# Stacked halves for decay and rate, and two reordered hand-ons, in an RWKV-7 / differential-attention trunk

## The chip, the cores and the metric

The kernel runs on one core of a Trainium2 chip. The metric is the device time of one launch in microseconds (us). Three runs of the kernel before gave 2142.01, 2142.14 and 2135.95 us, so their median is 2142.01. The profile is of one more execution, which took 2144.47 us; the trace of it spans 2142.8 us, with 1.67 us of the launch lying outside.

## The reference, cut to what matters

The program is a trunk of two layers on 512 tokens of 1024 channels in float32. Layer 0 is a feed-forward block, an RWKV-7 time mixing and another feed-forward block; layer 1 is the same with a differential attention in the middle. The change touches only the time mixing:

```python
r, k, v = jnp.einsum('sbtc,scd->sbtd', h[None] + dx[None] * mu[:3, None, None, :], w_rkv)
xw = h + dx * mu[3]; xa = h + dx * mu[4]; xg = h + dx * mu[5]
w_log = -jax.nn.softplus(-(w0 + jnp.tanh(xw @ w1) @ w2)) - 0.5
decay = jnp.exp(-jnp.exp(w_log))
a = jax.nn.sigmoid(a0 + (xa @ a1) @ a2)          # the "rate"
g = jax.nn.sigmoid(xg @ g1) @ g2                 # the gate, 160 inner channels
kk = (k * k_k).reshape(B, T, H, N)
kk = kk * lax.rsqrt(jnp.maximum(jnp.sum(kk * kk, axis=-1, keepdims=True), 1e-24))
k = k * (1 + (a - 1) * k_a)
y = wkv7_scan(heads(r), heads(decay), heads(k), heads(v), -kk, kk * a_h)   # heads of 64
```

w1, a1, w2 and a2 have an inner size of 64. Decay and rate are thus products over 64 channels, with 1024 outputs for each of 512 tokens.

## The kernel before, in words

Activations lie transposed: a tile has 128 channels on the partitions and the 512 tokens along the free axis, so 1024 channels are eight tiles, named 0 to 7. Every large product is computed in a split form. Each operand is cut into a high half (a cast to the 32-bit matmul format, by ScalarE) and a low half (the rest, a subtraction by VectorE), and `mm3` (lines 198 to 202) issues three matmuls of 512 columns for one product: high weights by high data (L200), high by low (L201), low by high (L202). Weights are cast at L146 and subtracted at L147 (`halves`), at L181/L182 (`wrows`, for the values) or at L194/L195 (`wflat`, for the small factors); activations at L207/L208 (`split`).

The program is traced with a tile scheduler. Within each engine it puts the instructions of independent pieces of the code into one fixed order before the launch, and each engine then runs its list strictly in that order; buffers come from pools with a fixed number of slots (`bufs`). `tc.issue_after(i)` tells this scheduler that what follows may not stand ahead of instruction `i`. The order on the chip is therefore a matter of the program alone, and an instruction that waits holds everything behind it in its list.

The time mixing runs in these steps, with their place in the trace of before:

- The low-rank inputs. `z` holds tanh(xw w1) on rows 0 to 63 and xa a1 on rows 64 to 127. Its halves are `zh`, `zl` (L603, L604). The gate's inner 160 channels are cut into 128 (`gh`, `gl`) and 32; the 32 go into a stacked tile `z3` of 96 rows.
- Decay, rate and gate, 400.75 to 417.66 us (loop from L674). For each of eight output tiles p and for each row half `hh` one `mm3` with 64 rows on both operands: rows 0 to 63 give decay, whose sigmoid goes to `A` (L681), rows 64 to 127 give rate, whose sigmoid goes to `BK` (L683). Three rounds later the gate's tile: one `mm3` of 128 rows and one 96-row matmul with `z3` (L689); VectorE copies the tile out of PSUM (L691).
- The mixing of v, k and r (`mixed`): for each of eight tiles a scaling of h (on VectorE at L654 for v, on ScalarE at L656 for k and r), a multiply-add on VectorE (L657), and a split (L207, L208).
- The values, 417.66 to 461 us, and beside them `rec(p)`, which turns decay into the factors of the recurrence: a scan on VectorE (L704) and more work on ScalarE and VectorE (L707 to L715).
- The key projection, from 461.3 us. `proj` (L209 to L251) computes two output tiles at a time from a block of 256 columns of the weights. When a tile is done it is put on the list `last`, and `hand_on` passes the tile that has waited there to the callback `done`. With `by_rows=b` the block at column b runs its products row by row, alternating between its two tiles. With `flush=False` the tile that is still on the list at the end is returned.
- The callback of the key projection is `key_done`: `key_cb` squares the tile on ScalarE (L755, into the tile `nacc`), a matmul with a block-diagonal matrix sums each head (L759), and a chain on ScalarE and VectorE normalises the key (L762 to L773, the last into `sA`). `scores(p - 2)` then moves a tile's rows into place by DMA (L786, `x<-sA`) and multiplies them (L794, L796). Last come steps of a triangular inversion on VectorE (`run(inv0, ...)`, L830 and L831).
- The receptance's projection R: its first block runs by rows with `feed(k)` between the products, which hands on key tile 7 and the scores of tiles 6 and 7. After it comes the recurrence proper (`wkv`).

## Time and profile before

| what | us |
|---|---|
| timed runs | 2142.01, 2142.14, 2135.95 |
| the profiled execution, and its span | 2144.47, 2142.8 |
| TensorE busy in the span | 2109.4 (98%) |
| VectorE, ScalarE busy | 1199.8 (56%), 816.7 (38%) |
| decay, rate and gate: TensorE from first to last start | 16.91 |
| gap between starts ahead of the first key tile's sum (L759) | 3.02 |
| gap between starts ahead of the last tile's scores (L794) | 1.75 |

How to read it: TensorE works nearly the whole span, so the time is the number of matmuls by their spacing, plus the places where TensorE stands. Matmuls are pipelined; the spacing of starts is what one costs, and the duration in a row is longer than that. The averages of the page hide the few places that the change touches, which the stretches and timelines show.

### The profile page before, as it was taken

What the parts mean: (1) busy time and instruction counts of PE and PEld (TensorE: products, weight loads), DVE (VectorE), ACT (ScalarE), POOL (GpSimd) and SP (SyncE); (2) the same over time, 40 slices, a digit from 0 to 9 for tenths busy, and PEclk for the clock granted to TensorE, in tenths of its full rate; (3) what the DMA queues carried; (4) which work ended last, traced back from release to release, by engine and by line L of the source; (5) the groups of instructions that cost most, each with busy time, mean ns of one, the idle gap of its engine ahead of it and who ended that gap; (6) DMA issues with size and microseconds to landing.
All of it is one profiled execution on the core that took longest, in us unless ns stands there. A gap on an engine that the chain in (4) does not pass through costs nothing.

```text
span 2142.8 us, 26517 instructions
## 1 busy us (share of the span) xinstructions
PE 2109.4 (98%) x10479; PEld 1771.9 (83%) x10479; DVE 1199.8 (56%) x1854; ACT 816.7 (38%) x1389; POOL 210.6 (10%) x250
## 2 busy tenths in 40 slices
PE   9999999999989999999999999999999999999999
PEld 7888888778789978888888988888889778888887
DVE  6644445797877764535446545445356855444443
ACT  5322223587235443323224342223235854222222
POOL 1100000000222201101000001001010210100000
PEclk9999999999989999999999999999999999999999
DMA  4333323346655542233223232333322113222222
GB/s 159 118 98 99 99 94 101 112 137 163 151 135 123 119 134 85 97 98 99 98 88 109 79 99 98 98 98 99 98 79 85 35 60 99 95 93 91 95 98 79
DMA packets 272920, 219.39 MB, mean 102 GB/s; under 512 B 85658, under 2 KB 257852, under 8 KB 272796
## 3 DMA queue, kind: packets, MB, share of 16 engines
q1 hardware_dynamic: 272796, 217.70, 33.5%
q8 instruction: 82, 1.34, 0.3%
q14 instruction: 42, 0.34, 0.0%
HBM read 193.02 MB, written 16.25 MB: 98 GB/s over the span
## 4 chain that ended last, share of the span: by engine, by line
PE 88%; DVE 6%; ACT 3%; DMA 1%; issue 1%; SPq 1%; POOL 0%; ACTq 0%; DVEq 0%
PE ps L200 27%; PE ps L202 27%; PE ps L201 27%; ACT s L1200 1%; PE ps L978 1%; PE ps L960 1%; PE ps L1004 1%; PE ps L966 1%; PE ps L993 1%; PE ps L988 0%; PE ps L972 0%; PE ps L995 0%; DVE wlo L147 0%; DVE s L1210 0%; DVE xmt L657 0%
## 5 line engine op out<-in xcount | busy, mean ns | idle before, releaser
L200 PE MATMUL ps<-xgh,whi 128*128 128x512 f32 x1688 | 658.4, 393 | 1.6 <-ACT whi L146 0.9
L201 PE MATMUL ps<-xgl,whi 128*128 128x512 f32 x1688 | 655.8, 390 | 0.0
L202 PE MATMUL ps<-xgh,wlo 128*128 128x512 f32 x1688 | 648.2, 390 | 0.1
L146 ACT CAST whi<-wraw 128x1024 fp32r<-128x1024 f32 (+2 forms) x296 | 303.5, 1030 | 880.3 <-PE ps L201 594.5
L147 DVE TENSOR_TENSOR wlo<-wraw,whi 128x1024 fp32r<-128x1024 f32 (+2 forms) x296 | 429.0, 1453 | 91.4 <-ACT whi L146 80.7
L200 PEld LDWEIGHTS ps<-xgh,whi 128*128 128x128 f32 x1688 | 316.4, 188 | 74.2 <-ACT whi L146 3.1
L201 PEld LDWEIGHTS ps<-xgl,whi 128*128 128x128 f32 x1688 | 316.9, 188 | 66.8 <-issue 1.7
L202 PEld LDWEIGHTS ps<-xgh,wlo 128*128 128x128 f32 x1688 | 316.6, 188 | 66.2 <-DVE wlo L147 0.6
L399 POOL TENSOR_TENSOR u<-u,g 128x512 f32<-128x512 f32 x88 | 124.7, 1418 | 1401.4 <-ACT whi L146 1114.4
L201 PE MATMUL ps<-actl,whi 128*128 128x512 f32 x656 | 255.2, 389 | 0.0
L200 PE MATMUL ps<-acth,whi 128*128 128x512 f32 x656 | 254.7, 389 | 0.0
L202 PE MATMUL ps<-acth,wlo 128*128 128x512 f32 x656 | 254.7, 389 | 0.0
L398 DVE TENSOR_TENSOR u<-ps,R 128x512 f32<-128x512 f32 x88 | 60.8, 691 | 286.6 <-PE ps L202 286.5
L441 DVE SCALAR_TENSOR_TENSOR x<-ps,x 128x512 f32<-128x512 f32 x88 | 60.5, 691 | 222.8 <-PE ps L202 222.8
L201 PEld LDWEIGHTS ps<-actl,whi 128*128 128x128 f32 x656 | 123.1, 188 | 25.6
L202 PEld LDWEIGHTS ps<-acth,wlo 128*128 128x128 f32 x656 | 123.1, 188 | 25.5
L200 PEld LDWEIGHTS ps<-acth,whi 128*128 128x128 f32 x656 | 123.1, 188 | 25.5
L200 PE MATMUL ps<-whi,xgh 128*128 128x256 f32 (+1 forms) x384 | 122.8, 323 | 0.2 <-DVE mx L1195 0.2
L201 PE MATMUL ps<-wlo,xgh 128*128 128x256 f32 (+1 forms) x384 | 122.5, 319 | 0.0
L202 PE MATMUL ps<-whi,xgl 128*128 128x256 f32 (+1 forms) x384 | 122.2, 318 | 0.0
L395 DVE TENSOR_TENSOR g<-ps,R 128x512 f32<-128x512 f32 x88 | 60.8, 691 | 108.2 <-PE ps L202 108.1
L207 ACT CAST acth<-u 128x512 fp32r<-128x512 f32 x88 | 54.8, 623 | 118.9 <-POOL u L399 118.8
(330 smaller groups left out, 2201.9 us busy)
## 6 DMA issues: line engine op xcount, KB each, us to landing
wraw<-in_ffn_w_in_dram SPq DMA_DIRECT2D x87, 1024.0 KB, 5.1
wraw<-in_ffn_w_out_dram SPq DMA_DIRECT2D x34, 1024.0 KB, 5.2
wraw<-in_rwkv_w_rkv_dram SPq DMA_DIRECT2D x12, 1024.0 KB, 5.7
wraw<-in_ffn_w_out_dram SPq DMA_DIRECT2D x12, 768.0 KB, 4.5
wraw<-in_w_kv_dram SPq DMA_DIRECT2D x8, 1024.0 KB, 5.0
am_d<-nsq SPq DMA_DIRECT2D x16, 256.0 KB, 2.9
AM<-am_d SPq DMA_DIRECT2D x16, 256.0 KB, 3.0
wraw<-in_diff_w_q_dram SPq DMA_DIRECT2D x4, 1024.0 KB, 5.4
```

The costliest lines, as they stand in the source:

```text
L146: self.nc.scalar.copy(hi[:, ks], raw[:, :, c : c + P])
L147: (eng or self.nc.vector).tensor_sub(lo[:, ks], raw[:, :, c : c + P], hi[:, ks].bitcast(F32))
L200: mm(ps, wh, xh, start=start, stop=False)
L201: mm(ps, wh, xl, start=False, stop=False)
L202: mm(ps, wl, xh, start=False, stop=stop)
L207: self.nc.scalar.copy(hi, src)
L395: nc.vector.tensor_mul(g, pg, self.R)
L398: nc.vector.tensor_mul(u, pu, self.R)
L399: nc.gpsimd.tensor_mul(u, u, g)
L441: nc.vector.scalar_tensor_tensor(x, ps, 0.5, x, ALU.mult, ALU.add)
L960: mm(pw[:, p, 0:L], Mo[:, p, :], DT[:, p, :].rearrange("p (h t) -> p h t", h=2)[:, :, 32:], start=True, stop=True)
L966: mm(p1[:, p, :], bbd[:, p, :], mv[:, p, :], start=True, stop=True)
```

## The change

There are three edits, in `proj`, in the decay and rate products, and in the mixing of the receptance.

The first: where the by-rows block is the last one and the list isn't flushed (the key projection), the two `hand_on` calls behind its products are left out, so two tiles, 6 and 7, stay on the list; `proj` returns the list, and `feed` hands on tile 6 at k = 0 and tile 7 at k = 1. (The call at k == 1 inside the by-rows loop, which hands on tile 5, stays.)

The second: the data tile for decay, `zw`, holds the high half of rows 0 to 63 of `z` on rows 0 to 63, and its low half on rows 64 to 127; `za` is the same for rate, the other way round. The weights `ww` hold the high half of w2 twice, one under the other, and `wa` that of a2. One matmul of 128 rows then gives high by high plus high by low, and one of 64 rows adds low by high. Three matmuls per product become two, 48 become 32. The weights of both are loaded twice, by two more DMAs, and there is one more cast of 128x1024 and one subtraction more of the weights; the split of `z` is two half-height copies and two half-height subtractions where there was one of each.

The third: ScalarE's scalings for the receptance may not stand ahead of the first key tile's square.

```diff
@@ proj
-                if not first or b:
+                if rows and not flush:
+                    pass
+                elif not first or b:
                     hand_on()
                 elif j == 0:
                     first()
                 last.append((b // P + j, pss[j]))
         if flush:
             hand_on()
-        return last[0] if last else None
+        return last
...
-            zh, zl = halves(z)
+            zw, za = (self.tl(self.gp, n, dt=F32R, bufs=XB) for n in ("xgh", "xgl"))
+            nc.scalar.copy(zw[half[0]], z[half[0]])
+            nc.vector.tensor_sub(zw[half[1]], z[half[0]], zw[half[0]].bitcast(F32))
+            nc.scalar.copy(za[half[1]], z[half[1]])
+            nc.vector.tensor_sub(za[half[0]], z[half[1]], za[half[1]].bitcast(F32))
...
-            def mixed(s, eng=None):
+            def mixed(s, eng=None, after=None):
...
-                        nc.scalar.activation(t, h[k][:, 1:], AF.Copy, scale=self.omu[:, i : i + 1])
+                        with tc.issue_after(after) if after else nullcontext():
+                            nc.scalar.activation(t, h[k][:, 1:], AF.Copy, scale=self.omu[:, i : i + 1])
...
-            wh, wl = self.wflat([(prm["w2"], 0), (prm["a2"], 64)], P)
+            ww, wa = (self.tl(self.wp, n, (P, 8, P), F32R, bufs=3).rearrange("p k f -> p (k f)") for n in ("whi", "wlo"))
+            wl = self.tl(self.wp, "wlo", (P, 8, P), F32R, bufs=3).rearrange("p k f -> p (k f)")
+            raw = self.tl(self.wp, "wraw", (P, 2, C), bufs=2)
+            for i, (w, n) in enumerate(((ww, "w2"), (wa, "a2"))):
+                for hh in half:
+                    nc.sync.dma_start(raw[hh, i], prm[n])
+                nc.scalar.copy(w, raw[:, i])
+                nc.vector.tensor_sub(wl[half[i]], raw[half[i], i], w[half[i]].bitcast(F32))
...
-            self.tl(self.wp, "wlo", (P, 8, P), F32R, bufs=3)
...
-                        self.mm3(ps, wh[hh, c], wl[hh, c], zh[hh], zl[hh], True, True)
+                        mm(ps, (ww, wa)[i][:, c], (zw, za)[i], start=True, stop=False)
+                        mm(ps, wl[hh, c], (zw, za)[i][hh], start=False, stop=True)
...
+            squares = []
+
             def key_cb(p, ps):
                 bb, kb = BK[:, p, :, 0:L], BK[:, p, :, L:]
                 sq = self.tl(self.gp, "nacc")
-                nc.scalar.activation(sq, ps, AF.Square, scale=self.v("k_k", p))
+                squares.append(nc.scalar.activation(sq, ps, AF.Square, scale=self.v("k_k", p)).ins)
...
-            xr = mixed(0)
+            xr = mixed(0, after=squares[0])

             def feed(k):
-                if k == 0:
-                    key_done(*last)
+                if k < 2:
+                    key_done(*last[k])
```

The lines below the edits move in the new file: L681, L683, L689 and L691 of before become L698, L700, L706 and L708; L755 and L759 become L774 and L778; L794 and L796 become L813 and L815; L656 and L657 become L665 and L666. The new products of decay and rate are L695 (128 rows) and L696 (64 rows).

TensorE's order within the decay, rate and gate stretch, before: rounds of three 64-row matmuls (data `xgh_2765`, `xgl_2766`), three 128-row matmuls of the gate (data `xgh_2800`), and the first two 96-row matmuls that finish a gate tile.

```order
L200 MATMUL ps_2920<-xgh_2800,whi_2850 128x512
L201 MATMUL ps_2920<-xgl_2801,whi_2850 128x512
L202 MATMUL ps_2920<-xgh_2800,wlo_2851 128x512
L200 MATMUL ps_2928<-xgh_2765,whi_2844 128x512
L201 MATMUL ps_2928<-xgl_2766,whi_2844 128x512
L202 MATMUL ps_2928<-xgh_2765,wlo_2845 128x512
L689 MATMUL ps_2902<-xgh_2834,whi_2854 128x512
L689 MATMUL ps_2920<-xgh_2834,whi_2854 128x512
L200 MATMUL ps_2933<-xgh_2765,whi_2844 128x512
```

The same place after, with the ninth decay and rate pairs; `wlo_2845` are the low weights, used with 64 rows.

```order
L695 MATMUL ps_2940<-xgh_2765,whi_2843 128x512
L696 MATMUL ps_2940<-xgh_2765,wlo_2845 128x512
L695 MATMUL ps_2944<-xgl_2766,wlo_2844 128x512
L696 MATMUL ps_2944<-xgl_2766,wlo_2845 128x512
L200 MATMUL ps_2948<-xgh_2802,whi_2857 128x512
L201 MATMUL ps_2948<-xgl_2803,whi_2857 128x512
L202 MATMUL ps_2948<-xgh_2802,wlo_2858 128x512
L706 MATMUL ps_2900<-xgh_2836,whi_2861 128x512
L706 MATMUL ps_2916<-xgh_2836,whi_2861 128x512
L706 MATMUL ps_2932<-xgh_2836,whi_2861 128x512
L706 MATMUL ps_2948<-xgh_2836,whi_2861 128x512
L695 MATMUL ps_2956<-xgh_2765,whi_2843 128x512
```

Each 64-row matmul (L696) now stands alone between matmuls of 128 rows, and the gate's first finishing matmul (L706 into `ps_2900`) has moved behind the decay and rate products of seven of the eight output tiles and behind four gate tiles' first three matmuls; before, its counterpart (L689 into `ps_2902`) stood behind those of five and a half output tiles and two gate tiles.

VectorE's order at the first copy of a gate tile, before: `xmt` are the mixing's intermediate tiles of v, `t_468` takes the gate's first tile.

```order
L644 TENSOR_TENSOR xgh_2834<-t_444_2828,xgh_2834 32x512
L208 TENSOR_TENSOR xgl_3010<-xmt_3006,xgh_3009 128x512
L208 TENSOR_TENSOR xgl_3017<-xmt_3013,xgh_3016 128x512
L654 TENSOR_SCALAR xmt_3020<-h_395_2578,omu 128x512
L654 TENSOR_SCALAR xmt_3027<-h_396_2579,omu 128x512
L691 COPY t_468_2907<-ps_2902 128x512
L657 SCALAR_TENSOR_TENSOR xmt_3020<-h_395_2578,vec_530,xmt_3020 128x512
L691 COPY t_472_2925<-ps_2920 128x512
```

And after:

```order
L652 TENSOR_TENSOR xgh_2836<-t_444_2830,xgh_2836 32x512
L208 TENSOR_TENSOR xgl_3000<-xmt_2996,xgh_2999 128x512
L708 COPY t_468_2905<-ps_2900 128x512
L708 COPY t_472_2921<-ps_2916 128x512
L208 TENSOR_TENSOR xgl_3007<-xmt_3003,xgh_3006 128x512
L662 TENSOR_SCALAR xmt_3010<-h_395_2578,omu 128x512
L662 TENSOR_SCALAR xmt_3017<-h_396_2579,omu 128x512
L666 SCALAR_TENSOR_TENSOR xmt_3010<-h_395_2578,vec_530,xmt_3010 128x512
```

The first copy of a gate tile stands three instructions earlier in the list of the mixing's work: ahead of one low half (`xgl_3007`) and of the two next scalings.

ScalarE's order around the first key tile's square, before: L656 are the receptance's scalings (`xmt_4048` and on), L146 a cast of weights, L755 the square into `nacc_3520`.

```order
L207 CAST xgh_3449<-xmt_3446 128x512
L207 CAST xgh_3456<-xmt_3453 128x512
L656 ACTIVATE xmt_4048<-h_393_2576,omu 128x512
L656 ACTIVATE xmt_4055<-h_394_2577,omu 128x512
L207 CAST xgh_4051<-xmt_4048 128x512
L207 CAST xgh_4058<-xmt_4055 128x512
L656 ACTIVATE xmt_4062<-h_395_2578,omu 128x512
L146 CAST whi_3547<-wraw_3541 128x1024
L755 ACTIVATE nacc_3520<-ps_3470,vec_530 128x512
L656 ACTIVATE xmt_4069<-h_396_2579,omu 128x512
```

And after, where the square is L774 into `nacc_3510` and the receptance's scalings are L665 into `xmt_3964` and on:

```order
L207 CAST xgh_3439<-xmt_3436 128x512
L207 CAST xgh_3446<-xmt_3443 128x512
L146 CAST whi_3537<-wraw_3531 128x1024
L774 ACTIVATE nacc_3510<-ps_3460,vec_530 128x512
L665 ACTIVATE xmt_3964<-h_393_2576,omu 128x512
L665 ACTIVATE xmt_3971<-h_394_2577,omu 128x512
L146 CAST whi_3668<-wraw_3666 128x1024
```

Between the key's last casts and the square there stands one cast of weights now, and no longer three scalings and two casts of the receptance beside it.

TensorE's order where the last key tile is handed on, before: L759 sums tile 7's heads, and the scores (L794, L796) and R's first products follow.

```order
L794 MATMUL ps_4010<-BK_2840,x_517_3065 128x128 x4
L796 MATMUL ps_4011<-ident,x_517_3065 128x128 x4
L759 MATMUL ps_4120<-nacc_4116,bd 128x512
L794 MATMUL ps_4136<-BK_2840,x_518_3066 128x128 x4
L796 MATMUL ps_4137<-ident,x_518_3066 128x128 x4
L794 MATMUL ps_4152<-BK_2840,x_518_3066 128x128 x4
L796 MATMUL ps_4153<-ident,x_518_3066 128x128 x4
L200 MATMUL ps_4114<-xgh_4051,whi_4106 128x512
```

And after, where that sum is L778 into `ps_4116`:

```order
L202 MATMUL ps_4031<-xgh_3981,wlo_4027 128x512
L200 MATMUL ps_4030<-xgh_3988,whi_4022 128x512
L201 MATMUL ps_4030<-xgl_3989,whi_4022 128x512
L778 MATMUL ps_4116<-nacc_4112,bd 128x512
L813 MATMUL ps_4132<-BK_2842,x_518_3056 128x128 x4
L815 MATMUL ps_4133<-ident,x_518_3056 128x128 x4
L813 MATMUL ps_4148<-BK_2842,x_518_3056 128x128 x4
```

The sum of tile 7 stands 20 of R's matmuls later than before; between tile 6's sum and it there now stand the scores of tile 4 and those 20.

## Rows read from the trace of the kernel before

**Rows 1.** The page: the span, and the chain that ended last by engine.

```profile
span 2142.8 us, 26517 instructions
...
PE 88%; DVE 6%; ACT 3%; DMA 1%; issue 1%; SPq 1%; POOL 0%; ACTq 0%; DVEq 0%
```

**Rows 2.** Stretches (us): length, each engine's busy time, TensorE's granted clock, DMA share, GB/s.

```profile
400.75:417.66 16.91, 16.27 (x82) 10.60 (x82) 12.88 (x22) 14.92 (x27) 0.00 (x0) 1.00 0.16 62
417.66:469.50 51.84, 51.84 (x229) 42.54 (x227) 51.73 (x71) 41.81 (x78) 1.92 (x2) 1.00 0.47 151
472.40:475.43 3.03, 0.40 (x3) 0.01 (x1) 2.72 (x4) 2.92 (x5) 0.48 (x2) 1.00 0.00 0
475.43:478.94 3.51, 3.51 (x7) 2.15 (x7) 3.12 (x5) 2.88 (x5) 0.00 (x0) 0.51 0.45 140
483.48:485.27 1.79, 1.79 (x7) 1.13 (x6) 1.55 (x3) 1.69 (x3) 0.00 (x0) 1.00 0.00 0
546.39:548.14 1.75, 0.39 (x3) 0.03 (x1) 1.69 (x5) 1.54 (x5) 0.00 (x0) 1.00 0.85 163
588.07:598.31 10.24, 9.41 (x44) 9.04 (x44) 8.22 (x23) 0.37 (x1) 0.00 (x0) 0.50 0.27 54
```

**Rows 3.** Timeline of TensorE, decay and gate: start, duration, line, tiles, shape, idle before.

```profile
400.75 1.19 PE L200 MATMUL ps<-xgh,whi 64*128 64x512 f32 x7
...
403.69 0.50 PE L200 MATMUL ps<-xgh,whi 128*128 128x512 f32 x1
404.03 0.40 PE L201 MATMUL ps<-xgl,whi 128*128 128x512 f32 x1
404.26 0.40 PE L202 MATMUL ps<-xgh,wlo 128*128 128x512 f32 x1
404.59 0.75 PE L200 MATMUL ps<-xgh,whi 64*128 64x512 f32 x2
...
406.63 0.50 PE L200 MATMUL ps<-xgh,whi 64*128 64x512 f32 x1
...
407.52 0.73 PE L689 MATMUL ps<-xgh,whi 96*128 96x512 f32 x2
408.89 0.50 PE L200 MATMUL ps<-xgh,whi 64*128 64x512 f32 x1 [0.64 <-ACT BK L683]
```

**Rows 4.** Timeline of VectorE, from the small factors to the key's tile 7.

```profile
409.89 0.69 DVE L691 COPY t<-ps 128x512 f32<-128x512 f32 x1
...
428.97 2.33 DVE L704 TENSOR_TENSOR_SCAN t<-rst,sA 128x512 f32<-128x512 f32 x2
...
469.48 1.36 DVE L208 TENSOR_TENSOR xgl<-xmt,xgh 128x512 fp32r<-128x512 f32 x2
...
541.89 0.68 DVE L773 TENSOR_TENSOR sA<-R,sR 128x512 f32<-128x512 f32 x1
```

**Rows 5.** Timeline of ScalarE ahead of the first key tile's square.

```profile
473.13 0.72 ACT L656 ACTIVATE xmt<-h,omu 128x512 f32<-128x512 f32 x1
473.76 1.03 ACT L146 CAST whi<-wraw 128x1024 fp32r<-128x1024 f32 x1
474.69 0.68 ACT L755 ACTIVATE nacc<-ps,vec 128x512 f32<-128x512 f32 x1
```

**Rows 6.** Timeline of TensorE, first key tiles, then the last tile's scores.

```profile
470.23 0.50 PE L201 MATMUL ps<-xgl,whi 128*128 128x512 f32 x1
...
475.43 2.08 PE L759 MATMUL ps<-nacc,bd 128*128 128x512 f32 x2 [2.63 <-ACT nacc L755]
...
530.53 1.02 PE L759 MATMUL ps<-nacc,bd 128*128 128x512 f32 x2
...
548.14 1.13 PE L794 MATMUL ps<-BK,x 128*128 128x128 f32 x8 [1.36 <-DVE x L831]
```

**Rows 7.** Timeline of SyncE's queue: the last tile's rows sent into place.

```profile
544.61 1.28 SPq L786 DMA_DIRECT2D x<-sA  x2
```

**Rows 8.** Timeline of ScalarE, the cast of the small factors.

```profile
367.03 1.06 ACT L194 CAST whi<-wraw 128x1024 fp32r<-128x1024 f32 x1 [4.43 <-DMA wraw<-in_rwkv_a_dram]
```

## The prediction, written before the result was known

> **What bounds the kernel now.** The page comes first: TensorE is 88% of the chain that ended last over a span of 2142.8 us [rows 1], so a change counts where it alters what TensorE issues or where TensorE stands. The stretches come next, because the change touches some 160 us of the span and the page's means say nothing of them. Values and the key's first products run without a hole: 229 matmuls in 51.84 us, 0.2264 us from start to start, at the full clock, while VectorE is busy 51.73 of 51.84 us [rows 2]. There TensorE sets the time, with VectorE just keeping up. Behind that comes a hole of 3.03 us, ended by the first key tile's square, and then seven matmuls in 3.51 us at a granted clock of 0.51, the lower level (1.2 of 2.4 GHz); the same seven take 1.79 us further on at the upper level [rows 2]. A last hole of 1.75 us stands ahead of the last key tile's scores, and the clock stayed up there [rows 2, 6]. Last the timelines: which instruction ended each hole, and what stood ahead of it on its engine.
>
> **Decay and rate.** 48 matmuls become 32 and the gate's 32 stay, so 64 take the place of 80 in a stretch of 16.91 us [rows 2]. Counted at 0.2264 us each, 16 fewer would save 3.6 us. The timeline speaks against that count. While only half-row matmuls run, the decay's (rows 0 to 63) and the rate's (rows 64 to 127) run side by side: seven of them start within the 0.81 us to the next row, and the whole run of 24 at the stretch's start takes from 400.75 to 403.69, 2.94 us or 0.12 us each [rows 3]. So a half-row matmul costs half where it has its partner. And a change of height costs extra: three 128-row matmuls start at 403.69 and the next half-row one at 404.59, 0.90 us for 0.68 us of streaming; three half-row ones start at 406.63 and the 96-row one at 407.52, 0.89 us [rows 3]. Each visit to the other height is thus some 0.21 us dearer, part ahead of its first matmul and part behind it: 404.03 minus 403.69 is 0.34, not 0.23 [rows 3].
>
> After, each of the 16 half-row matmuls stands alone between full-row ones, which makes 32 changes of height. 64 x 0.2264 = 14.5 us, and 32 x 0.21 = 6.7: 21.2 us against 16.91, so +4.3 us. The bounds: nothing per change gives 14.5 (-2.4); if a lone matmul overlaps neither neighbour it costs its whole 0.50 us [rows 3], 16 x 0.50 on top of 48 x 0.2264 plus 0.21 per return, 22.2 (+5.3). I take +4.3, which is the row's own figure. The wait of 0.64 us for a sigmoid at 408.89 [rows 3] is already in the 16.91, and goes; it is repaid by nothing, since the changes are counted afresh.
>
> The Trainium skill says under TensorEngine Tiling (Array Packing), Key Properties, that "Changing tiling mode (not just tile) drains the TensorE" while different tiles work in parallel; this trace agrees with both, 0.21 us a visit and pairs at 0.12 us each.
>
> The additional loads (two DMAs of 256 KB on SyncE's queue), cast and subtraction fall near 367 us, where ScalarE stood 4.43 us before the cast of 1.06 us [rows 8]. I set them at 0; without that cover the cast delays the rest by 1.1 us, the upper bound. The split of z grows by two half-height instructions on each engine in place of one; I count it into the same bound.
>
> **VectorE behind it.** The first copy of a gate tile started at 409.89 us [rows 4]; it waits for that tile's 96-row matmul, and the multiply-adds of v's mixing, then the scans, queue behind it. After, 40 matmuls with 28 changes lie ahead of this 96-row matmul: 400.75 + 40 x 0.2264 + 28 x 0.21 = 415.7, plus 0.5 for the matmul: 416.2, 6.3 us later. From it to the scan VectorE ran 19.1 us (428.97 minus 409.89 [rows 4]); after, four more instructions lie between, one low half, two scalings and a 1.1 us weight subtraction, some 2 us more by my estimate from VectorE's 0.69 us for a tile [rows 4]. The scan comes 8.3 us later. The subtraction was only moved, so 7.1 us remains at the key's last low halves (469.48 [rows 4]). VectorE has 0.11 us of idle time in that stretch [rows 2] to catch up. TensorE comes 4.3 us later, so it would wait 2.8 us for the key's mixing where it now waits some tenths (470.23 lasts 0.50 [rows 6]). I take +2.8; bounds 0 (VectorE's first copy not held back) and +4.
>
> **The first square.** The square began at 474.69, behind a cast at 473.76 and a receptance scaling at 473.13 [rows 5], and TensorE waited 2.63 us for it [rows 6]. After, no scaling stands ahead of it and the cast can run while TensorE finishes the tile. What remains is the square itself, 0.68 us [rows 5], and a hand-over of 0.1: the hole of 3.03 becomes 0.8, -2.2 us; bounds 0 and -2.8. Held back are ScalarE's scalings for the receptance and their splits, which R needs some 55 us later. Then the slow clock behind the hole: 3.51 minus 1.79 is 1.72 us. A hole of 1.75 us left the clock at 1.00 [rows 2]; 0.8 us, and the 2.8 us ahead of it in pieces of one low half each, are nearer to that than to 3.03. I take -1.7; the bound is 0.
>
> **The last hand-ons.** Tile 7's sum moves behind 20 of R's matmuls, 4 us later than 530.53 [rows 6]. Its scores stood at 548.14 [rows 6], behind the send issued at 544.61 [rows 7], behind the last vector step at 541.89 [rows 4], 11.4 us after the sum, most of it queueing behind the inversion's steps. I expect scores at 548.3 on the old scale. The sends of tile 5's scores, which its hand-on issues on SyncE's queue, move with it by the same 4 us and stay ahead of the last send. But five of R's matmuls that ran behind the scores now stand ahead of them, so R's next block starts about 1.0 us earlier: -1.0. If tile 7 needs its old 17.6 us from sum to scores, they start at 552.1, which is +3; if it needs no wait at all, -1.5.
>
> **The sum.** +4.3 +2.8 -2.2 -1.7 -1.0 = +2.2 us on the profiled execution's 2144.47, which is 2146.7. That execution lies 2.46 us above the median of the runs, so 2144.2 us on their scale. A measurement here tells 0.3% (6.4 us) from no change; the forecast is no change.
>
> **Rivals.**
> 1. VectorE becomes the bound (slower). In the key's block it is wanted for weight halves and for the key's chain. If the 7.1 us that it is late aren't given back at the first square, because the key's tile then waits for VectorE's next weight half, neither the -2.2 nor the -1.7 is earned, and with the last hand-on at its bound of +3 for the same reason, the sum is +4.3 + 2.8 + 3 = +10.1: 2152.1 us. For it: 51.73 of 51.84 us busy. Against it: behind the first square VectorE holds less of the receptance's mixing. It decides from the point where VectorE is more than 4 us late against TensorE.
> 2. Height changes are hidden (faster): a lone half-row matmul's weights are loaded while the full-row one streams, and the changes cost nothing. Then -2.4 for the stretch, VectorE about level (0), -2.2, -1.7, -1.0: -7.3, or 2134.7 us. Against it: 0.90 and 0.89 us for three.
> The Trainium skill's TensorE: Matmul & The Clock Gate, Part 3, The mechanism, lets the engine pull a weight load ahead of running matmuls where the rows don't conflict or the background buffer is free; by that rule the time is this rival's. The trace disagrees: 0.21 us per visit were paid.
> 3. The square waits as before, for the cast of weights or its slot: no -2.2 and no -1.7. The sum is +6.1: 2148.1 us.
>
> **Chances.** Forecast 0.52, its own range 2140 to 2148; rival 1 0.18; rival 2 0.13; rival 3 0.17. Faster by over 0.3% (under 2135.6) gets most of rival 2, 0.11. Slower (over 2148.4) gets rival 1, some of rival 3 and a tail of the forecast: 0.24. Within 0.3%: 0.65. The range that leaves out 2 in 10 is 2136.5 to 2151.
>
> **What would show it.** The decay and rate stretch at about 21 us, with 0.44 us for each lone half-row matmul, shows the first term; under 17 us, rival 2. The first gate copy at about 416 and the scan at about 437 show the second, with small waits for low halves at the key's start. A hole under 1.2 us ahead of the first key sum and a clock of 1.00 behind it show the third and fourth; a hole over 2.5 us is rival 3. R's second block about 1 us nearer to the last key sum of tile 6 shows the fifth. The forecast is wrong if the stretch of 400 to 480 us is longer or shorter by over 6 us than worked out here.

## The result: slower by 0.57%, and the profile after

The changed kernel takes 2152.28 us in the median of five runs (2148.63 to 2156.47), against 2142.01 before. The ratio, taken over all the runs, is 1.0057 with a 95% interval of 1.0037 to 1.0078 (the two medians alone give 1.0048). Forecast was no change, 2144.2 us, with 2136.5 to 2151 as the range that leaves out 2 in 10. The measured time lies above it, so the forecast is wrong; slower was given a chance of 0.24.

The traced execution of the changed kernel is its fastest, 2148.63 us, and that of the kernel before was among its slowest: of 29 further runs before, the median is 2138.92. The two traces differ by 4.2 us, the medians by 10.3, so the traces are read stage by stage and not by their ends. The page after, its span and the chain that ended last:

```profile
span 2146.9 us, 26483 instructions
...
PE 87%; DVE 6%; ACT 3%; DMA 1%; issue 1%; SPq 0%; POOL 0%; ACTq 0%; DVEq 0%
```

Stretches of the kernel after: length, busy time of TensorE, its weight loads, VectorE, ScalarE and GpSimd, the granted clock, DMA share and GB/s.

```profile
400.58:421.76 21.18, 21.18 (x65) 11.55 (x64) 10.04 (x16) 16.02 (x26) 0.00 (x0) 1.00 0.10 38
421.76:480.03 58.27, 55.94 (x241) 44.41 (x239) 56.08 (x78) 43.48 (x81) 3.03 (x4) 1.00 0.45 149
480.03:481.46 1.43, 0.39 (x2) 0.00 (x1) 0.61 (x1) 1.43 (x3) 0.00 (x0) 1.00 0.00 0
494.67:499.09 4.42, 0.60 (x2) 0.03 (x1) 4.38 (x8) 3.09 (x5) 0.00 (x0) 1.00 0.81 228
499.09:502.50 3.41, 3.41 (x16) 3.41 (x17) 2.13 (x4) 0.89 (x3) 0.00 (x0) 0.51 0.44 82
```

The first is decay, rate and gate: 21.18 us for 16.91 [rows 2]. The third answers to the hole of 3.03 us ahead of the first key sum [rows 2]; it is 1.43 now. The fourth is new: TensorE stands 4.42 us, and behind it comes the lower clock, 0.51, which before stood behind the first key sum. The timeline of TensorE at these places:

```profile
400.90 0.50 PE L696 MATMUL ps<-xgh,wlo 64*128 64x512 f32 x1
401.33 0.49 PE L695 MATMUL ps<-xgl,wlo 128*128 128x512 f32 x1
401.75 0.49 PE L696 MATMUL ps<-xgl,wlo 64*128 64x512 f32 x1
...
475.32 0.50 PE L201 MATMUL ps<-xgl,whi 128*128 128x512 f32 x1 [1.29 <-DVE xgl L208]
...
481.46 1.12 PE L778 MATMUL ps<-nacc,bd 128*128 128x512 f32 x2 [1.04 <-ACT nacc L774]
...
499.09 1.99 PE L813 MATMUL ps<-BK,x 128*128 128x128 f32 x8 [3.82 <-DVE BK L776]
```

Each lone half-row matmul and each full-row one beside it starts 0.43 us behind the last: the pair costs 0.85 us where two full-row ones cost 0.45. At 475.32 and 499.09 are the two waits that the kernel before does not have there. The rows of the weight loads (PEld) in the same stretch are:

```profile
400.90 0.18 PEld L696 LDWEIGHTS ps<-xgh,wlo 64*128 64x128 f32 x1 [0.36 <-issue]
401.33 0.19 PEld L695 LDWEIGHTS ps<-xgl,wlo 128*128 128x128 f32 x1 [0.25 <-issue]
```

Each of them starts together with its own matmul. So it is for 32 of the 64 matmuls of the stretch, as many as there are changes of height; the loads of the others start 0.23 us ahead of their matmul. At full height (e7 below) 63 of 64 do. A load that is not hidden is thus where these rows show the price of a change, and rival 2, by which it would be hidden, falls.

In a table, the time of TensorE from mark to mark in the traces (start of the first matmul of each stage), with the deferral (the third edit) and the stacking (the second) marked; the runs e1 to e14 are the experiments below, and e8 is left out because it repeats e7.

| kernel | stacked | deferral | decay, rate, gate | to first key sum | to tile 3's sum | to tile 6's | to the recurrence |
|---|---|---|---|---|---|---|---|
| before | no | no | 16.91 | 57.77 | 23.40 | 28.08 | 59.68 |
| after | lone | yes | 21.18 | 59.70 | 27.48 | 28.08 | 57.89 |
| e11, after again | lone | yes | 25.40 | 59.70 | 27.45 | 28.08 | 58.14 |
| e1 | lone | no | 31.33 | 59.81 | 21.80 | 28.09 | 58.27 |
| e5 | lone | no | 24.05 | 59.99 | 21.81 | 28.09 | 58.25 |
| e12, e5 again | lone | no | 31.37 | 60.09 | 21.78 | 28.09 | 57.85 |
| e2 | no | yes | 18.38 | 55.63 | 27.24 | 28.08 | 58.36 |
| e4 | no | yes | 16.91 | 56.19 | 27.32 | 28.08 | 57.57 |
| e3 | no | no | 16.91 | 57.75 | 23.42 | 28.08 | 57.43 |
| e6 | full height | yes | 15.21 | 60.29 | 27.54 | 28.09 | 57.32 |
| e7 | full height | no | 15.22 | 59.90 | 21.80 | 28.08 | 57.78 |
| e10 | pairs | no | 16.20 | 60.44 | 21.78 | 28.08 | 57.10 |
| e13 | full height | no | 15.43 | 60.36 | 21.81 | 28.08 | 58.50 |
| e14 | no | no | 16.94 | 58.50 | 23.40 | 28.08 | 58.08 |
| e9 | no | later | 18.38 | 55.63 | 21.78 | 31.16 | 58.19 |

Up to the recurrence the trace after is 8.5 us longer than that before: +4.3, +1.9, +4.1, 0, -1.8. Behind that, the recurrence takes 167.0 us for 171.6, since its clock was up in more of it in that one execution:

```profile
594.91:761.95 167.04, 154.19 (x1255) 147.14 (x1256) 128.00 (x316) 80.16 (x195) 41.23 (x51) 0.98 0.56 128
```

against this in the kernel before:

```profile
586.60:758.20 171.60, 160.98 (x1255) 154.19 (x1256) 128.96 (x315) 80.22 (x195) 41.51 (x51) 0.93 0.54 125
```

### The profile page after: what moved, and what is told of

Read it like the earlier page. It is cut to its first block, busy times and chain, and to the rows that moved or that the text cites. A ratio compares the mean times of both kernels' runs of the same rounds, so it can differ in the third digit from the quotient of the medians.

```text
span 2146.9 us, 26483 instructions
## 1 busy us (share of the span) xinstructions
PE 2109.7 (98%) x10463; PEld 1766.4 (82%) x10463; DVE 1199.5 (56%) x1856; ACT 818.4 (38%) x1391; POOL 209.0 (10%) x250
## 4 chain that ended last, share of the span: by engine, by line
PE 87%; DVE 6%; ACT 3%; DMA 1%; issue 1%; SPq 0%; POOL 0%; ACTq 0%; DVEq 0%
PE ps L200 27%; PE ps L202 27%; PE ps L201 27%; ACT s L1219 1%; PE ps L1023 1%; DVE wlo L147 1%; PE ps L997 1%; DVE x L850 0%; PE ps L979 0%; DVE t L721 0%; PE ps L1007 0%; PE ps L985 0%; PE ps L1014 0%; PE ps L1012 0%; ACT whi L146 0%
## 5 line engine op out<-in xcount | busy, mean ns | idle before, releaser
L146 ACT CAST whi<-wraw 128x1024 fp32r<-128x1024 f32 (+2 forms) x296 | 303.4, 1029 | 883.4 <-PE ps L201 603.2
L147 DVE TENSOR_TENSOR wlo<-wraw,whi 128x1024 fp32r<-128x1024 f32 (+2 forms) x296 | 429.8, 1456 | 94.3 <-ACT whi L146 81.8
L207 ACT CAST acth<-u 128x512 fp32r<-128x512 f32 x88 | 54.8, 623 | 118.9 <-POOL u L402 118.8
```

The lines of the kernel that those rows point to most:

```text
L146: self.nc.scalar.copy(hi[:, ks], raw[:, :, c : c + P])
L147: (eng or self.nc.vector).tensor_sub(lo[:, ks], raw[:, :, c : c + P], hi[:, ks].bitcast(F32))
L207: self.nc.scalar.copy(hi, src)
```

## The experiments

Where did the 4.42 us come from? Theory A says from the deferral, which put the receptance's work into key tile 0's chain. Theory B says from VectorE's lateness, thus from the stacking (computing decay and rate from stacked halves). The edits were run apart, each against the kernel before on the same chip.

**e1, the second edit alone**, with what goes with it; `proj`, `feed` and `mixed` as before.

```diff
-                        self.mm3(ps, wh[hh, c], wl[hh, c], zh[hh], zl[hh], True, True)
+                        mm(ps, (ww, wa)[i][:, c], (zw, za)[i], start=True, stop=False)
+                        mm(ps, wl[hh, c], (zw, za)[i][hh], start=False, stop=True)
```

> Only the stacked products for decay and rate; the hand-ons and the receptance's mixing are as before. Both theories: the stretch of decay, rate and gate takes about 21.2 us (16.91 before), and VectorE comes to the key's mixing some 7 us late. Theory A (the deferred mixing moved the hole: the receptance's work now stands behind the first square, inside tile 0's key chain): no hole over 1 us ahead of tile 0's scores, first key sum at 481 to 484, the sum of key tile 3 at 504 to 507 (498.8 before), the time 4 to 8 us above before. Theory B (VectorE's lateness from the stacking makes that hole): a hole of about 4 us ahead of tile 0's scores here too, tile 3's sum at 508 or later, the time 8 to 12 us above before.

Measured: 2149.92 us, ratio 1.0051 (1.0035 to 1.0068). No hole ahead of tile 0's scores, as theory A says; tile 3's sum comes 112.9 us behind the start of decay (98.1 before), most of it by something that neither theory had: the stretch itself took 31.33 us, at the lower clock for most of it.

```profile
405.00:428.50 23.50, 23.50 (x43) 12.45 (x43) 7.92 (x13) 11.30 (x18) 0.00 (x0) 0.50 0.09 33
```

**e2, the third edit alone.**

```diff
-            xr = mixed(0)
+            xr = mixed(0, after=squares[0])
```

> Only the receptance's scalings held behind the first square. Theory A: the hole ahead of the first key sum falls from 3.03 to about 1.4 us and the clock stays up behind it, but a hole of 3 to 4.5 us stands ahead of tile 0's scores, and tile 3's sum is at 498 to 501 (498.8 before): no gain, within 2 us of before. Theory B: no hole over 1 us ahead of tile 0's scores, tile 3's sum at about 495.5, the time 3 to 4 us under before.

Measured: 2143.18 us, ratio 1.0016 (1.0007 to 1.0025). The hole ahead of the first key sum is 1.43 us, and one of 4.39 us between starts stands ahead of tile 0's scores, with no stacking in the kernel:

```profile
491.66 1.62 PE L797 MATMUL ps<-BK,x 128*128 128x128 f32 x6 [3.80 <-DVE BK L760]
```

Theory B falls. Theory A expected no gain, within 2 us; it is a loss of 4.3 by the medians and 3.4 by the ratio (1.5 to 5.3 within its interval).

**e3, the first edit alone.**

```diff
+                if rows and not flush:
+                    pass
...
-                if k == 0:
-                    key_done(*last)
+                if k < 2:
+                    key_done(*last[k])
```

> Only the later hand-on of key tiles 6 and 7. Both theories: nothing changes before tile 6's sum; from there to the first matmul of the recurrence it takes 57.5 to 58.5 us (59.7 before, 57.9 with the whole change), so 1 to 2 us under before in the trace and no difference that the runs can tell.

Measured: 2138.32 us, ratio 0.9994 (0.9984 to 1.0004). From tile 6's sum to the recurrence 57.43 us, as expected. But e1 and e2, which do not have this edit, also need only 58.3 us there, so the edit's own part is smaller than the difference to 59.68. TensorE's wait ahead of the recurrence's first matmul tells it better: 1.5 to 1.8 us in the three traces without this edit (before, e1, e2), 0.7 to 1.0 in the thirteen with it.

**e4, the first and the third.**

> The change without the stacked products. Theory A: as the deferral alone (a hole of 3 to 4.5 us ahead of tile 0's scores) and 1 to 2 us less behind tile 6's sum; the time -3 to +1 us against before. Theory B: no such hole, and the time 4 to 6 us under before. In both the 16.91 us of decay, rate and gate stay, and the kernel is some 6 us or more faster than with the whole change.

Measured: 2141.45 us, ratio 1.0012 (1.0003 to 1.0020). The hole of 4.48 us is there, and the row names what it waits for, the rows of tile 0's `sA` sent into place by DMA:

```profile
490.36 0.98 PE L799 MATMUL ps<-BK,x 128*128 128x128 f32 x3 [3.89 <-DMA x<-sA]
```

Expected was 6 us or more under the whole change; by the medians it is 10.8 under it, by the two ratios to before 9.6.

What holds that DMA up is read in the whole change's trace. ScalarE, from the cast ahead of the first square (L774) to the normaliser's root (L783):

```profile
479.77 1.05 ACT L146 CAST whi<-wraw 128x1024 fp32r<-128x1024 f32 x1 [1.93 <-PE ps L201]
480.73 0.68 ACT L774 ACTIVATE nacc<-ps,vec 128x512 f32<-128x512 f32 x1
481.31 1.32 ACT L665 ACTIVATE xmt<-h,omu 128x512 f32<-128x512 f32 x2
482.53 1.04 ACT L146 CAST whi<-wraw 128x1024 fp32r<-128x1024 f32 x1
483.48 0.68 ACT L781 ACTIVATE t<-ps,bias 128x512 f32<-128x512 f32 x1
484.06 0.68 ACT L774 ACTIVATE nacc<-ps,vec 128x512 f32<-128x512 f32 x1
484.63 1.14 ACT L207 CAST xgh<-xmt 128x512 fp32r<-128x512 f32 x2
485.78 1.28 ACT L783 ACT_TABLE_LOAD   x1
487.07 0.72 ACT L783 ACTIVATE t<-t,bias 128x512 f32<-128x512 f32 x1
```

Two scalings of the receptance and two of its casts (L665, L207) stand between the square and the root at 487.07; in e7, without the deferral, it is one of each. VectorE's part of the chain, up to the last step of tile 0:

```profile
487.83 0.75 DVE L784 SCALAR_TENSOR_TENSOR t<-ps,vec,t 128x512 f32<-128x512 f32 x1 [0.89 <-ACT t L783]
...
489.11 0.75 DVE L666 SCALAR_TENSOR_TENSOR xmt<-h,vec,xmt 128x512 f32<-128x512 f32 x1
...
490.38 0.75 DVE L666 SCALAR_TENSOR_TENSOR xmt<-h,vec,xmt 128x512 f32<-128x512 f32 x1
491.04 1.22 DVE L147 TENSOR_TENSOR wlo<-wraw,whi 128x1024 fp32r<-128x1024 f32 x1
...
492.78 0.69 DVE L792 TENSOR_TENSOR sA<-t,sR 128x512 f32<-128x512 f32 x1
```

Two more of the receptance's steps (L666) lie within it, and a subtraction of weights (L147) that stands behind `sA` in e7. From the first key sum to the end of `sA` it takes 12.0 us (481.46 to 493.47), and so it does in all five traces with this edit (after, e2, e4, e6, e11); in e7 it takes 9.3 us, in the ten others 8.2 to 9.3. Last SyncE's queue, in which a row with x2 covers two issues:

```profile
482.11 10.55 SPq L135 DMA_DIRECT2D wraw<-in_rwkv_w_rkv_dram  x2
493.53 6.20 SPq L805 DMA_DIRECT2D x<-sA  x4
```

The second of the weight loads, 1 MB, is issued at the end of its row, 492.7, just ahead of tile 0's send. From the first issue of the send to the last signal that it has landed it takes 5.4 us (498.96; TensorE starts 0.13 us behind it). The kernel without the deferral, e7 below, has its weights behind the send:

```profile
485.72 1.38 SPq L799 DMA_DIRECT2D x<-sA  x2
487.20 0.57 SPq L135 DMA_DIRECT2D wraw<-in_rwkv_w_rkv_dram  x1
```

whose last signal comes at 489.26, 3.5 us behind the issue, and TensorE runs into the scores without a wait:

```profile
490.01 1.05 PE L807 MATMUL ps<-BK,x 128*128 128x128 f32 x8
```

Over e7 the chain is 2.7 us longer and the send 1.9, together 4.6. Less the 0.75 us by which the send was early in e7 (489.26 to 490.01), that is the 3.82 us for which TensorE waits in the row at 499.09. The send takes 5.4 to 5.5 us in each of the five traces with the edit, and 3.5 in each of the others.

(The row at 499.09 above names VectorE's L776, which ended at 498.98; a wait for several semaphores is put down to the one that came last, and those two came within 0.02 us.)

The second question is the clock in e1. Theory C: changes of height also bring the clock down, in most executions. Theory D: they cost their own 0.21 us each and nothing more.

**e5, the first and second edits, without the deferral.**

> The whole change without the deferral of the receptance's scalings. Theory A (the deferral makes the hole ahead of tile 0's scores): no hole over 1 us there, and from the end of the gate to the recurrence 166 to 167.5 us (173.4 with the whole change, 168.2 with the stacked products alone). On what is left of the loss, theory C (the lone half-row matmuls also bring the clock down in their stretch, in most executions): the time 2146 to 2150. Theory D (only the height changes' 4.3 us and VectorE's lateness): 2139 to 2142.

Measured: 2149.37 us, ratio 1.0046 (1.0034 to 1.0059): theory C's time. The hole ahead of the scores is gone, from the end of the gate to the recurrence it takes 168.1 us (expected 166 to 167.5). The order on every engine is that of e7 below, with the height of 16 matmuls as the only difference.

```profile
401.08:425.13 24.05, 24.05 (x66) 12.82 (x65) 10.00 (x16) 16.22 (x26) 0.00 (x0) 0.86 0.09 33
```

**e6, the whole change at full height.**

```diff
-                        mm(ps, wl[hh, c], (zw, za)[i][hh], start=False, stop=True)
+                        mm(ps, wl[:, c], (zw, za)[i], start=False, stop=True)
```

> The whole change, with one edit: the second product of decay and rate takes all 128 rows of its weights and data, so that no height changes are left, and as many matmuls as before; it adds low by low of the other factor's weights, which is of the size of what the split leaves out anyway. If the height changes are the cost (theories C and D): the stretch of decay, rate and gate takes 14.5 to 15 us (21.2 with the whole change), at the full clock. By theory A the hole of about 4.4 us ahead of tile 0's scores is still there, and the time is 2138 to 2140. If it were the stacking itself, or VectorE's later start, that costs: the stretch stays over 18 us and the time over 2145.

Measured: 2145.99 us, ratio 1.0036 (1.0023 to 1.0050). The instructions and their order are those of the whole change; only the height of 16 matmuls differs. The stretch falls from 21.18 to 15.21 us at the full clock:

```profile
399.49:414.70 15.21, 14.91 (x66) 11.96 (x64) 9.25 (x15) 14.86 (x26) 0.00 (x0) 1.00 0.12 45
```

The hole of 4.42 us ahead of tile 0's scores is still there. The stretch is near the first expectation, but the time is 6 to 8 us above it and within what was expected if the stacking itself costs. In part it does: from the end of the gate to the first key sum it takes 60.29 us, where e4, without the stacking, takes 56.19.

**e7, full height without the deferral.**

> As the full-height kernel, without the deferral. Theory A: no hole over 1 us ahead of tile 0's scores, the hole ahead of the first key sum is back at 1.5 to 3 us; stretch of decay, rate and gate 14.5 to 15 us; the time 2134 to 2137, below before by 2 to 4 us. By the rival (the deferral is what pays) it would be no faster than the full-height kernel with it.

Measured: 2139.93 us, ratio 1.0006 (0.9997 to 1.0015), 6.1 us under e6 and so the price of the deferral in this pair; but 3 to 6 us more than expected. (Between e4 and e3, without the stacking, the price is 3.1 us; between the whole change and e5 it is 2.9, across two sessions.) Up to the recurrence its trace is 3.1 us shorter than that of before; that gain is not in the time. The hole ahead of the first key sum is 1.55 us between starts, and the clock behind it stays at 1.00, though nothing is deferred here:

```profile
476.34 1.12 PE L772 MATMUL ps<-nacc,bd 128*128 128x512 f32 x2 [1.16 <-ACT nacc L768]
```

So it is in every kernel with the stacking and without the deferral, with holes of 1.29 to 1.56 us in e1, e5, e8, e10 and e12 and 1.88 in e13.

**e8, full height, the scalings held behind tile 0's last vector step.**

```diff
+                steps.append(nc.vector.tensor_mul(ch(A[:, p, :]), k3, Rb[:, p, :, 0:L]).ins)
...
+            xr = mixed(0, after=steps[0])
```

> As the full-height kernel, but the receptance's scalings wait for the last vector step of key tile 0 and not for its square. Theory A: both holes shrink, the one ahead of the first key sum to about 1.4 us and the one ahead of tile 0's scores to under 1 us; the time 2130 to 2134. Rival: the work that is put off only opens a hole elsewhere, ahead of the scores of a later tile or of the receptance's first products, and the time is 2136 or more.

Measured: 2139.82 us, ratio 1.0012 (1.0003 to 1.0020). It tested nothing: the instruction named belongs to another engine than the scalings, and the order on every engine came out as that of e7, so it is a second measurement of e7.

**e9, hand-ons, and the scalings held behind ScalarE's last step of tile 0's chain**, with decay and rate as before; `squares` holds this step now.

```diff
+                squares.append(nc.scalar.activation(t, rs, AF.Square, scale=math.sqrt(0.5)).ins)
...
+            xr = mixed(0, after=squares[0])
```

> Decay and rate as before, the later hand-ons, and the receptance's scalings held behind the last ScalarE step of key tile 0's chain instead of its square. Theory A (the deferral costs because the receptance's work stands inside tile 0's chain): the hole ahead of the first key sum is about 1.4 us as with the deferral alone, the hole ahead of tile 0's scores falls from 4.4 to under 1.5 us, from the end of the gate to the recurrence 164 to 165.5 us (169.2 before), and the time 2134 to 2137. Rival (TensorE has nothing to fill the chain's time with, wherever the receptance's work stands): a hole of 3 us or more ahead of tile 0's scores or of tile 1's, the time 2139 or more.

Measured: 2142.81 us, ratio 1.0017 (1.0008 to 1.0026). Tile 0's chain is free (9.0 us), and 21.78 us to tile 3's sum show it; then tile 1's scores wait, with 3.42 us between starts:

```profile
500.04 1.13 PE L799 MATMUL ps<-BK,x 128*128 128x128 f32 x8 [2.83 <-DMA x<-sA]
```

The rival's hole and time came, but what made the hole is read on SyncE's queue:

```profile
492.07 0.59 SPq L791 DMA_DIRECT2D x<-sA  x1
...
496.72 0.47 SPq L816 DMA_DIRECT2D mo_d<-nr_a  x1
497.24 1.99 SPq L791 DMA_DIRECT2D x<-sA  x3
```

Tile 1's rows are sent in two halves. Its chain ends at 492.00 (11.2 us behind its sum, 7.9 in e7, with the receptance's work in it), and the first half goes at 492.07. The second half goes at 497.24, behind eight sends of tile 0's scores, and its last signal comes at 499.90. With both halves sent at 492.1 and the 3.5 us of e7 there would be no hole, as an estimate: the rows would have been in place at 495.6, and tile 3's sum, the matmul ahead of the scores, starts at 496.61. In before, the receptance's work stood ahead of the first square, with a hole of 3.03 us and the lower clock behind it [rows 2].

**e10, pairs.** Both full-row matmuls, then both half-row ones, in the kernel without the deferral.

```diff
+                    pss = [self.ps(), self.ps()]
+                    for i in range(2):
+                        full = mm(pss[i], (ww, wa)[i][:, c], (zw, za)[i], start=True, stop=False)
+                    for i, hh in enumerate(half):
+                        with tc.issue_after(full.ins):
+                            mm(pss[i], wl[hh, c], (zw, za)[i][hh], start=False, stop=True)
```

> The stacked products without the deferral, with the half-row matmuls of decay and rate put next to each other, so that 16 changes of height are left of 32. Stretch of decay, rate and gate: 16.1 us if the two of a pair run side by side, 17.9 if not (21.2 lone, 15.2 at full height). Theory C (changes of height also bring the clock down): the time 2141 to 2146, between the full-height kernel's 2139.9 and the lone ones' 2149.4, with the clock falling in the stretch in some executions. Theory D (only their own 0.21 us each): 2139 to 2141.5.

Measured: 2139.54 us, ratio 1.0002 (0.9993 to 1.0010): theory D's time, for 16 changes. In its one trace the stretch takes 16.20 us at the full clock, and a pair's two matmuls start together:

```profile
401.49 0.50 PE L694 MATMUL ps<-xgh,wlo 64*128 64x512 f32 x1
401.49 0.50 PE L694 MATMUL ps<-xgl,wlo 64*128 64x512 f32 x1
```

This trace has the lower clock elsewhere, from 472.6 to 476.0, behind a wait for a low half at the key's start that is longer here than in the other kernels; it is in the 60.44 us of the table:

```profile
471.15 0.50 PE L201 MATMUL ps<-xgl,whi 128*128 128x512 f32 x1 [2.80 <-DVE xgl L208]
```

**e11 and e12, the whole change and e5 once more**, one execution each.

> The changed kernel once more, for the clock in the stretch of decay, rate and gate in another execution. Theory C: a granted clock of 0.5 for a part of the stretch, which then takes more than 21.2 us. Theory D: 1.00 and 21.2 us, as in the first trace of it.

> The change without the deferral once more, for the clock in the same stretch. Theory C: a clock of 0.5 for a part of it, as in its first trace (24.05 us). Theory D: 1.00 and 21.2 us.

Measured: 2154.92 and 2155.59 us. In e11 the stretch takes 25.40 us, of which:

```profile
405.00:415.20 10.20, 10.20 (x17) 4.68 (x17) 1.38 (x2) 6.42 (x11) 0.00 (x0) 0.50 0.00 0
```

and in e12 31.37 us:

```profile
400.02:431.39 31.37, 31.37 (x65) 16.76 (x64) 11.04 (x17) 16.25 (x26) 0.00 (x0) 0.62 0.09 34
```

So of five traces with lone half-row matmuls (after, e1, e5, e11, e12), four lost the clock in that stretch, and it grew by 2.9 to 10.2 us; of the five traces at full height or with pairs none did. The old order lost it too, for 3.4 us, in two traces of six (e2 and e9, 18.38 us each), so it is not the stacking's alone. Theory C is borne out for lone ones, on few executions, and what in the alternation brings the clock down is not shown.

**e13 and e14, the gate's copies on ScalarE**, in e7 and in e3. The question was whether VectorE's lateness sets when the key's first tiles end.

```diff
-                    nc.vector.tensor_copy(t, ps)
+                    nc.scalar.copy(t, ps)
```

> The full-height kernel without the deferral (2139.93 us, 59.9 us from the end of the gate to the first key sum), with one edit: ScalarE and not VectorE copies the eight gate tiles out, some 4.8 us of VectorE's work. Theory E (VectorE's lateness sets when the key's first tiles end): the waits of TensorE for low halves at the key's start (1.68 us the longest) go, and the 59.9 us fall by 1.5 us or more; the time 2136 to 2138.5. Rival (the key's start is set by ScalarE or the weights, and VectorE is only busy): the 59.9 us stay within 0.5, and the time 2139 or more.

> Decay and rate as before the change, the later hand-ons, and the gate's copies on ScalarE. Theory E: there TensorE hardly waits for VectorE at the key's start (0.4 us in the trace of before), so only up to 0.5 us is to be had from the end of the gate to the first key sum (57.75 with the later hand-ons alone), if the square does not come later on a busier ScalarE; the time 2137 to 2140. Rival to both: ScalarE's sigmoids wait behind the copies and decay, rate and gate takes over 17.5 us (16.91).

Measured: 2139.30 us, ratio 0.9992 (0.9983 to 1.0001), and 2140.79, ratio 1.0001 (0.9992 to 1.0010). In e13 the way to the first key sum takes 60.36 us, not less than 59.90, and the wait at the key's start stays:

```profile
471.84 0.50 PE L201 MATMUL ps<-xgl,whi 128*128 128x512 f32 x1 [1.42 <-DVE xgl L208]
```

These are the rival's numbers. But the edit did not make VectorE earlier, so it did not test theory E. In e7 VectorE is busy 23.95 of the 24 us from 416 to 440, in e13 20.09. It now stands there for ScalarE's cast, and ahead of the scan (the first two rows are e13's, the last is e7's):

```profile
428.18 0.69 DVE L208 TENSOR_TENSOR xgl<-xmt,xgh 128x512 fp32r<-128x512 f32 x1 [2.19 <-ACT xgh L207]
...
433.08 2.34 DVE L717 TENSOR_TENSOR_SCAN t<-rst,sA 128x512 f32<-128x512 f32 x2 [1.46 <-issue]
```

```profile
432.61 2.33 DVE L717 TENSOR_TENSOR_SCAN t<-rst,sA 128x512 f32<-128x512 f32 x2
```

The scan starts 33.0 us behind the start of decay in e13 and 31.4 in e7. Theory E stays open. In e14 the same way takes 58.50 us (57.75 in e3), as its expectation allowed. No kernel here is faster than the one before beyond its interval; the nearest are e3 and e13.

## Why the prediction was wrong, step by step

**Decay and rate: the size was right at the full clock, the clock was not.** 21.2 us were worked out, and the first trace has 21.18. The sum took the clock of before's row, 1.00 [rows 2], for the new stretch too, and no rival let it fall. It fell in four of five traces, and e6, in which nothing but the height differs, has 15.21 us at 1.00. On the mean of the five traces this term is 26.7 minus 16.9, +9.8 us instead of +4.3. That mean overstates the median run: e1's traced execution took 2155.01 us with a median of 2149.92. In time, e5 against e7, where only the height differs, makes it 9.4 us for 6.0 at the full clock; the whole change against e6 makes it 6.3, across two sessions. So how much of the 10 us is the clock's stays open.

**VectorE behind it: near.** The first copy was forecast at 416.2 and the scan at 437.3; the trace has these:

```profile
415.83 1.29 DVE L708 COPY t<-ps 128x512 f32<-128x512 f32 x2 [3.24 <-PE ps L706]
...
437.84 2.33 DVE L721 TENSOR_TENSOR_SCAN t<-rst,sA 128x512 f32<-128x512 f32 x2
```

TensorE lost 3.3 us over the key's first two tiles (14.6 us from 465.65 to 480.26, against 11.3 from 461.33 to 472.63 before), for 2.8 forecast. The rows name VectorE's low halves there (475.32), and VectorE is busy for all of the 30 us from 440 to 470; that its late first copy is the cause, as the step says, stays open, since e13 did not move it.

**The first square: gained, but less, and not by the edit that was credited.** The hole is 1.43 us, not 0.8, because the cast of weights ahead of the square waited 1.93 us for TensorE, in ScalarE's row at 479.77, and could not run while the tile was being finished. Together with the step above the way to the first key sum was forecast 0.6 us longer, and is 1.9 longer. The prediction took the wait for VectorE and the hole as separate terms. In the stacked kernels without the deferral the hole is already 1.55 us and the clock stays up behind it (e1, e5, e7), so with the stacking the deferral brings 0.1 us at the hole, and to the first key sum 0.3 us (59.70 against 59.99 in e5) or nothing (60.29 in e6 against 59.90 in e7). Without the stacking it brings 2.1 us there (e2, 55.63 for 57.77).

**The deferral counted at no cost: this step failed, and the slow clock's gain with it.** The prediction said that what is held back are scalings and splits "which R needs some 55 us later", so it cost them nothing. They were put where the key's chain runs, and e2 shows the price without any stacking: 4.39 us ahead of tile 0's scores, with 3.4 us at the lower clock behind it in each of the traces with this edit (after, e2, e4, e6, e11). From the first key sum to tile 3's sum -1.7 us was forecast and +4.1 measured; without the deferral it is -1.6 (e1, e5, e7: 21.8 for 23.40), so the slow clock was indeed saved there, and the deferral spent it again. In time, e6 against e7 makes the deferral's price 6.1 us and the whole change against e5 2.9, with the stacking; e2 against before makes it 4.3 without. Forecast was a gain of 3.9 (2.2 and 1.7), so this is the step with the largest miss.

**The last hand-ons: right in sign.** -1.0 was forecast and -1.8 measured in the whole change; but the kernels without this edit show -1.3 to -1.4 there, so it is not the edit's alone; some 0.8 us of it is, by the wait ahead of the recurrence's first matmul.

**Rival 1** gave 2152.1 us, which is the time measured, by luck: it had the hole ahead of the first square as long as before and the last tile's scores late. The hole was shorter and the clock stayed up behind it, and tile 0's scores were late.

**What stays open.** Up to the recurrence, e7 and e10 are 2 to 3 us shorter than before in their traces, and their times are the same or 1.8 us longer. The traced execution of e7 is also the slowest of its eleven. One trace holds one execution, and the recurrence alone differs by more than that between two executions shown above (167.0 and 171.6 us). Why every stacked kernel needs 1.9 to 2.7 us more than before to the first key sum, and what in alternating heights brings the clock down, is not shown either.

## What to carry to other kernels

Fewer matmuls are not less time where their heights alternate: count the changes and look at what runs side by side, and either pair the half-height ones or give all of them the full height. (Here that only took the loss away: neither kernel is faster than the one before.) Work that is put off goes somewhere in a list that is served in order: before it is counted at nothing, read what stands behind its new place, on every engine that it uses and on the DMA queue.

## What the runs showed of the hardware that was not expected

A stretch in which TensorE never stood still by the profile (24.05 us busy of 24.05 in e5, 31.37 of 31.37 in e12) lost its clock: at alternating heights, in four of five executions, for 6.8 to 23.9 us, and never there in the five traces with 16 changes of height or none (e6, e7, e8, e10, e13). The ends of matmuls are modelled, so the busy time doesn't exclude short idle spells. In the Trainium skill's TensorE: Matmul & The Clock Gate, HAM oscillation, the throttle comes back where the engine waits for a DMA; the section behind it, A second HAM failure mode, has it come back through short idle spells between groups of matmuls. The second is nearer to what these runs show, but no row here shows an idle spell in that stretch; whether the weight loads that start with their own matmul (400.90) make such spells, no row tells.

And the time of a small transfer depends on what was issued ahead of it: tile 0's send took 3.5 us from issue to the last signal of its landing in e7, and 5.4 us in the whole change, where the issue of 1 MB of weights had ended 0.9 us before it.
